# Attention block: probabilities scaled by the reciprocal of their sum, gate rows summed by four matmuls into one tile, last output tile in two column parts

## The chip, the cores and the metric

The kernel runs on one core of a Trainium2 chip. The metric is the device time of one execution in microseconds; the figure compared is the median over runs. A core has TensorE (PE, matmuls; PEld is its weight load), VectorE (DVE), ScalarE (ACT), GpSimd (POOL), and SyncE (SP), which issues the transfers here.

## The reference

One layer of a hybrid block with 2048 channels, 512 latent tokens and 256 context tokens. One input projection feeds eight heads of a gated delta rule (a scan) and eight heads of attention (two key/value heads, 768 keys). Both outputs are multiplied by a SiLU gate and pass through one output projection; its result, times a gate row, is added to x, and a final RMSNorm follows.

```python
def attend(q_blk, k_all, v_all):
    s = jnp.einsum('bqkgd,bskd->bkgqs', q_blk, k_all) * (HEAD_DIM ** -0.5)
    p = jax.nn.softmax(s, axis=-1)
    return jnp.einsum('bkgqs,bskd->bqkgd', p, v_all)

mod = jax.nn.silu(c) @ w_ada[l] + b_ada[l]
shift, scale, gate = jnp.split(mod, 3, axis=-1)          # 2048 channels each
...
attn_lat = block_attention(qa, k_all, v_all) * jax.nn.silu(z_a)
y = jnp.concatenate([gdn_lat, attn_lat], axis=-1) @ w_out
x = x + gate * y
return rms_norm(x, final_norm_w)
```

## The kernel before

Float32 products are built from two parts of each factor: hi is the value rounded to the matmul's format (a cast on ACT), lo the rest (a subtraction on DVE), and a product is three matmuls (hi hi, hi lo, lo hi), which is the helper mm3. Each weight piece of 256 KB is loaded by SP (wraw), cast on ACT (whi, L129), and its rest formed on DVE (wlo, L130). Names follow: whi_z and wlo_z belong to the gate projection z, whi_wo and wlo_wo to the output projection.

The program has a prologue (context and latent normalised, the modulation formed), the scan of the delta rule up to about 876 us, the attention stage from about 876 to 1114 us, then the output projection in four column blocks of 512, with four token tiles of 128 rows in each. The change lies in the attention stage and in the last column block.

The attention stage runs over units u = 0 to 16. Unit u = 2h + qp takes head h and the 256 queries qp; even units have qp = 0, odd ones qp = 1. Here "its unit" is the one whose scores are made, and "the unit before" is the one whose probabilities are used. In a unit stand, in the order of the code:

- attn_pt for the unit before: the probabilities pr (128 queries x 768 keys, two tiles) are transposed on PE, in three groups (pt), and each is split on ACT (pth) and DVE (ptl).
- attn_scores: the scores s in PSUM, and the row maximum on DVE (mx).
- attn_spread for the unit before: a matmul of ones with the diagonal tile dg puts 1/sum of each query on all partitions (ov), and ACT copies it to SBUF.
- attn_exp: two ACT operations make pr from s, with the sum of each row as their second output.
- fill(FS, 2): four steps of the generator of z matmuls (zl, 512 columns, three per step), and two steps of the gate row. A step of z matmuls at the start of a piece issues the casts and subtractions of a later weight piece. A step of the gate row (gate_rows) multiplies a 256 KB piece of w_ada by a scalar per partition and adds it to gacc on DVE (L1402).
- fill(FV, 2), then attn_values for the unit before: 18 matmuls of 256 columns (o), and on DVE the product of o, of ov and, where the gate of the head is known already ("early": M then holds it), of M.
- for the first five units the tanh and SiLU of a gate made earlier (zae, L1455).
- at an even unit attn_norm of the next head's queries (the copy qn, L1230); at an odd unit attn_qt: the next head's queries transposed (qtp) and split into qTh (ACT, L950) and qTl (DVE, L951), which the next unit's scores need.
- attn_over: the reciprocal of the row sums and dg, both on DVE.

PSUM tiles pt, ov, qtp share a ring of two places. The z matmuls and the sums of the gate row share another (pl).

The order of ACT, DVE and POOL in this stage is the order of the code (a manual schedule), and PE's has been written out too; SP issues its loads as their buffers come free. Every 512 columns of the gate row, gate_out sums gacc over the 128 partitions with a matmul of ones into 32 partitions (gater), adds the bias row on DVE and writes the 2 KB to memory (grd): three times inside the stage, from the z filler, once at its end. The epilogues read grd back as gbc.

In the last column block, for each token tile t, po3 is 48 matmuls of 512 columns; the epilogue multiplies by gbc (tt), adds x (yx), squares with a sum (fss) and multiplies by the final norm's weight fwb. Then DVE reduces the four sums, POOL takes the power -0.5 (fr), ACT and DVE scale one half of the row (1024 columns) each, and SP writes each half.

Of the kernel before, what the change touches and what calls it, by code (L numbers as in the profile page):

```python
# [68 lines left out]
def build(tc, a):  # L69
# [1202 lines left out]
            prs.append(pr)  # L1272
        return prs

    def attn_over(h, qp, mx):

        dg = ap_.tile([128, 2, 128], F32, tag="dg", bufs=2, name=f"dg{h}_{qp}")
        V.reciprocal(mx[:, 1], mx[:, 1])
        V.tensor_tensor(out=dg, in0=ident.unsqueeze(1).to_broadcast([128, 2, 128]),
                        in1=mx[:, 1].unsqueeze(2).to_broadcast([128, 2, 128]), op=ALU.mult)  # L1280
        return dg

    def attn_pt(h, qp, prs, j2):

# [8 lines left out]
        split_from(tp3, pth, ptl)  # L1293
        return pth, ptl

    def attn_spread(h, qp, dg):

        ov = ttile([128, 256], f"ov{h}_{qp}")
        T.matmul(ov, lhsT=ones, rhs=dg.rearrange("p a b -> p (a b)"), start=True, stop=True)
        over = ap_.tile([128, 256], F32, tag="ov", bufs=2, name=f"ov{h}_{qp}")  # L1300
        S.copy(over, ov)
        return over

    def attn_values(h, qp, pts, over):
        kv = h // 4
        op = PSt.tile([128, 256], F32, tag="o", name=f"o{h}_{qp}")
        for j in range(6):
            vsl = slice(kv * 128, kv * 128 + 128)
            mm3(op, vah[:, j, vsl], val[:, j, vsl], pts[j // 2][0][:, j % 2], pts[j // 2][1][:, j % 2], j == 0, j == 5)
        m = M[8 + h][:, qp * 256:qp * 256 + 256]  # L1310
        if (h, qp) in early:
            V.scalar_tensor_tensor(out=m, in0=m, scalar=0.5, in1=over, op0=ALU.mult, op1=ALU.mult)
# [31 lines left out]
    def fillers():  # L1344

        pieces = [z_piece(0), z_piece(1)]
        over = None
        yield
        for n in range(4 * len(zs)):
            i, kq = zs[n // 4], n % 4  # L1350
            if n + 2 < 4 * len(zs):
                pieces.append(z_piece(n + 2))
            if kq == 2 and outs:
                gate_out(*outs.pop(0))
            hi, lo = pieces.pop(0)
            if kq == 0:
                pl = PP.tile([128, SEQ], F32, tag="pl", name=f"zl{i}")
            for k4 in range(4):
                k = kq * 4 + k4
                for m, (lw, rt) in enumerate(((hi[:, k4], hhL[:, k]), (hi[:, k4], hl(0, k)), (lo[:, k4], hhL[:, k]))):  # L1360
                    T.matmul(pl, lhsT=lw, rhs=rt, start=k == 0 and m == 0, stop=k == KT - 1 and m == 2,  # L1361
                             skip_group_check=True)
# [6 lines left out]
    def gate_out(c, acc, row):

        pr = PP.tile([128, 512], F32, tag="pl", name=f"gater{c}")
        T.matmul(pr[0:32], lhsT=ones[:, 0:32], rhs=acc, start=True, stop=True)
        V.tensor_tensor(out=row, in0=row, in1=pr[0:1], op=ALU.add)
        SY.dma_start(grd[:, c * 512:c * 512 + 512], row)

    outs = []

    def gate_rows():

        def load(i):  # L1380
            c, k = divmod(i, KT)
            raw = ap_.tile([128, 512], F32, tag="graw", bufs=GB, name=f"graw{i}")
            SY.dma_start(raw, w_ada[k * 128:(k + 1) * 128, 2 * D + c * 512:2 * D + c * 512 + 512])
            return raw

        def bias(c):
            row = ap_.tile([128, 512], F32, tag="ze", bufs=2, name=f"grow{c}")[0:1]
            SY.dma_start(row, a["b_ada"][:, 2 * D + c * 512:2 * D + c * 512 + 512])
            return row

        raws = [load(i) for i in range(GB - 1)]
        acc = last = None
        yield
        for i in range(4 * KT):
            c, k = divmod(i, KT)
            raw = raws.pop(0)
            if k == 0:
                last, acc = acc, ap_.tile([128, 512], F32, tag="gacc", bufs=2, name=f"gacc{c}")
            if k == 0:
                V.tensor_scalar(out=acc, in0=raw, scalar1=scol[:, k:k + 1], scalar2=None, op0=ALU.mult)  # L1400
            else:
                V.scalar_tensor_tensor(out=acc, in0=raw, scalar=scol[:, k:k + 1], in1=acc, op0=ALU.mult, op1=ALU.add)  # L1402
            if i + GB - 1 < 4 * KT:
                raws.append(load(i + GB - 1))
            if k == 3 and c:
                outs.append((c - 1, last, bias(c - 1)))
            yield
        outs.append((3, acc, bias(3)))

    qcs = {i: attn_q(i) for i in (1, 2)}  # L1410
    for i in range(8):
# [21 lines left out]
    for u in range(2 * NH + 1):  # L1433
        h, qp = divmod(u, 2)
        more = h + 1 < NH
        prs, pts = None, []
        if before is not None:
            pts = [attn_pt(before[0], before[1], before[2], j2) for j2 in range(2)]
        if h < NH:
            sos, mx = attn_scores(h, qp, *qt, scs[h])  # L1440
        if before is not None:
            pts.append(attn_pt(before[0], before[1], before[2], 2))
            over = attn_spread(before[0], before[1], dg)
        if h < NH:
            prs = attn_exp(h, qp, sos, mx, scs[h])
            if qp == 1 and more:
                qn = next(qns)
            fill(FS + 5 * (before is None), 2)
        if before is not None:
            fill(FV, 2)  # L1450
            attn_values(before[0], before[1], pts, over)
        if u < NZA:

            e = ap_.tile([128, SEQ], F32, tag="ze", bufs=2, name=f"zae{u}")
            S.activation(e, M[8 + u], AF.Tanh, scale=0.5)  # L1455
            silu(V, M[8 + u], M[8 + u], e)
            early.update(((u, 0), (u, 1)))
        fill(FQ)
        if more:
            if qp == 0:  # L1460
                qns = attn_norm(h + 1, qcs.pop(h + 1))
                next(qns)
                if h + 3 < NH:
                    qcs[h + 3] = attn_q(h + 3)
            else:
                qt = attn_qt(h + 1, qn)
        if h < NH:
            dg = attn_over(h, qp, mx)
# [63 lines left out]
    for c in range(4):  # L1532
        cs_ = slice(c * 512, c * 512 + 512)
        for t in range(4):
            SY.dma_start(yx[:, t, cs_], a["x"][0, t * 128:t * 128 + 128, cs_])
        if c < 3:
            if c:
                ops = out_block(c)
            for t in range(4):
                epilogue(c, t, ops[t])  # L1540
            continue
        for k in range(KT):
            hi = op_.tile([128, 512], F32R, name=f"wlh{k}")
            lo = op_.tile([128, 512], F32R, name=f"wll{k}")
            raw = op_.tile([128, 512], F32, tag="rawl", bufs=2, name=f"rawl{k}")
            SY.dma_start(raw, w_out[k * 128:(k + 1) * 128, cs_])
            S.copy(hi, raw)
            V.tensor_tensor(out=lo, in0=raw, in1=hi, op=ALU.subtract)
            wlast.append((hi, lo))
        for t in range(4):  # L1550
            ts_ = slice(t * 128, t * 128 + 128)
            ps = PO.tile([128, 512], F32, tag="po", name=f"po3_{t}")
            for k in range(KT):
                mm3(ps, mh[k][:, ts_], ml[k][:, ts_], *wlast[k], k == 0, k == KT - 1)
            epilogue(c, t, ps)
            f = fr[:, t:t + 1]
            V.tensor_reduce(out=f, in_=fss[:, t], axis=AX.X, op=ALU.add)
            V.tensor_scalar(out=f, in0=f, scalar1=1.0 / D, scalar2=EPS, op0=ALU.mult, op1=ALU.add)
            power(f, -0.5)
            for q in range(2):  # L1560
                qs = slice(q * 1024, q * 1024 + 1024)
                if q == 0:
                    S.activation(yx[:, t, qs], yx[:, t, qs], AF.Copy, scale=f)
# [29 lines left out]
```

## Time and profile before

| what | value |
|---|---|
| runs | 1305.47, 1527.16 and 1306.19 us, median 1306.19 |
| profiled execution, own time | 1304.42 us |
| its span | 1302.6 us |
| mean granted TensorE clock | 0.993 |
| busy PE / PEld | 1250.4 us (96%) / 1018.4 us (78%) |
| busy DVE / ACT / POOL | 842.5 us (65%) / 583.4 us (45%) / 141.9 us (11%) |
| matmuls | 9226 |

The own time is that of the execution that was profiled; the span goes from its first to its last record. Rows of the order of time, below, read: start in us, duration in us, engine, source line, operation, output <- inputs, shapes, number of operations put together, and in brackets the idle time of the engine before it and what ended it. Grouped rows of waits read: engine and line that waited, for whom: us in total, times, longest. Rows of DMA issues read: count, KB each, us from issue to landing.

### The profile page before, as it was taken

How to read it: one execution, taken by the hardware profiler on the slowest of the kernel's cores; microseconds unless marked ns; L12 is line 12 of the kernel's file. 1: busy time of each engine (PE TensorE's matmuls, PEld its weight loads, DVE VectorE, ACT ScalarE, POOL GpSimd, SP SyncE). 2: the span in 40 equal slices, each digit the busy share in tenths (PEclk: the TensorE clock that was granted, in tenths of full speed). 3: DMA queues.
4: the chain of work that ended last, by engine and by line, in shares of the span. 5: the costliest groups of instructions: out<-in, count | busy, mean ns of one | idle time of the engine just before them, and what ended most of it. 6: DMA issues, size and time to landing. Idle time of an engine off the chain costs nothing. (4 is left out here: it accounts for less than half of the span.)

```text
span 1302.6 us, 24348 instructions
## 1 busy us (share of the span) xinstructions
PE 1250.4 (96%) x9226; PEld 1018.4 (78%) x9226; DVE 842.5 (65%) x1893; ACT 583.4 (45%) x1464; POOL 141.9 (11%) x206
## 2 busy tenths in 40 slices
PE   6799999999999999999999999999999999999997
PEld 4466688888888888888888877787888888788885
DVE  5444596686867678675776646537888887555432
ACT  4222363455545454544545444535555444434211
POOL 1323100111111111111111001100000000000000
PEclk9999999999999999999999999999999999999998
DMA  9999424231332313222132443356443443475302
GB/s 354 316 326 347 133 67 107 60 67 55 74 72 62 78 47 83 67 69 57 54 83 75 106 131 110 99 164 214 149 129 114 123 140 102 161 244 190 93 33 97
DMA packets 227000, 164.53 MB, mean 126 GB/s; under 512 B 62210, under 2 KB 198491, under 8 KB 225859
## 3 DMA queue, kind: packets, MB, share of 16 engines
q1 hardware_dynamic: 226586, 162.87, 42.9%
q8 instruction: 73, 1.20, 0.4%
q14 instruction: 44, 0.36, 0.1%
q10 hardware_dynamic: 297, 0.11, 0.0%
HBM read 148.85 MB, written 14.08 MB: 125 GB/s over the span
## 5 line engine op out<-in xcount | busy, mean ns | idle before, releaser
L240 POOL TENSOR_TENSOR sdh<-sth,egl 128x256 f32<-128x256 f32 x80 | 56.9, 711 | 446.6 <-DVE sth L892 344.8
L871 ACT ACTIVATE oqh<-ksh,egsw 64x128 f32<-64x128 f32 x128 | 46.3, 362 | 92.7 <-DVE rh L866 86.4
L866 DVE SCALAR_TENSOR_TENSOR rh<-ksh,negeg,vtokh 64x128 f32<-64x128 f32 x176 | 61.2, 348 | 31.1 <-PE ksh L854 24.5
L146 PE MATMUL po<-whi_wo,mh 128*128 128x512 f32 x192 | 76.2, 397 | 0.0
L148 PE MATMUL po<-whi_wo,ml 128*128 128x512 f32 x192 | 76.1, 396 | 0.0
L147 PE MATMUL po<-wlo_wo,mh 128*128 128x512 f32 x192 | 76.1, 396 | 0.0
L1361 PE MATMUL zl<-hhL,whi_z 128*128 128x512 f32 x176 | 74.0, 421 | 0.0
L1361 PE MATMUL zl<-hhL,wlo_z 128*128 128x512 f32 x176 | 69.8, 396 | 0.0
L1361 PE MATMUL zl<-hL,whi_z 128*128 128x512 f32 x176 | 69.6, 395 | 0.0
L130 DVE TENSOR_TENSOR wlo_wo<-wraw_wo,whi_wo 128x512 fp32r<-128x512 f32 x48 | 33.0, 690 | 55.5 <-ACT whi_wo L129 55.3
L886 PE MATMUL tsh<-vsh,ktok 128*128 128x128 f32 x352 | 56.6, 283 | 6.7 <-ACT vnh L882 3.5
L886 PEld LDWEIGHTS tsh<-vsh,ktok 128*128 128x128 f32 x352 | 47.4, 190 | 16.0 <-ACT vnh L882 7.9
L129 ACT CAST whi_wo<-wraw_wo 128x512 fp32r<-128x512 f32 x48 | 29.6, 620 | 67.3 <-PE po L148 56.8
L892 DVE TENSOR_TENSOR sth<-sdh,tsh 128x256 f32<-128x256 f32 x80 | 33.6, 420 | 27.4 <-PE tsh L886 19.2
L879 ACT ACTIVATE vsh<-tsh,cch 128x128 f32<-128x128 f32 x88 | 32.2, 366 | 38.4 <-PE tsh L875 37.1
L164 PE MATMUL vl<-hhL,wlo_v 128*128 128x512 f32 x112 | 46.3, 413 | 0.0
L164 PE MATMUL vl<-hhL,whi_v 128*128 128x512 f32 x112 | 46.2, 413 | 0.0
L164 PE MATMUL vl<-hL,whi_v 128*128 128x512 f32 x112 | 45.8, 409 | 0.0
L1402 DVE SCALAR_TENSOR_TENSOR gacc<-graw,scol,gacc 128x512 f32<-128x512 f32 x60 | 44.9, 748 | 1.0
L950 ACT CAST pth<-pt 128x512 fp32r<-128x512 f32 x48 | 26.8, 585 | 40.7 <-PE pt L1289 40.7
L146 PEld LDWEIGHTS po<-whi_wo,mh 128*128 128x128 f32 x192 | 36.2, 188 | 9.5 <-ACT whi_wo L129 0.8
L148 PEld LDWEIGHTS po<-whi_wo,ml 128*128 128x128 f32 x192 | 36.2, 189 | 8.7
(540 smaller groups left out, 3890.2 us busy)
## 6 DMA issues: line engine op xcount, KB each, us to landing
wada<-in_w_ada SPq DMA_DIRECT2D x64, 512.0 KB, 8.6
graw<-in_w_ada SPq DMA_DIRECT2D x64, 256.0 KB, 3.1
wraw_wo<-in_w_out SPq DMA_DIRECT2D x48, 256.0 KB, 3.3
wraw_z<-in_w_in SPq DMA_DIRECT2D x44, 256.0 KB, 3.1
wraw_v<-in_w_in SPq DMA_DIRECT2D x28, 256.0 KB, 2.9
wraw_k<-in_w_in SPq DMA_DIRECT2D x24, 256.0 KB, 2.9
wraw_q<-in_w_in SPq DMA_DIRECT2D x24, 256.0 KB, 2.8
xs<-in_x SPq DMA_DIRECT2D x4, 1024.0 KB, 5.4
```

What stands on the lines that cost most here:

```text
L130: (lo_eng or G).tensor_tensor(out=lo, in0=raw, in1=hi, op=ALU.subtract)
L146: T.matmul(out, lhsT=lh, rhs=rh, start=start, stop=False, skip_group_check=True)
L147: T.matmul(out, lhsT=lh, rhs=rl, start=False, stop=False, skip_group_check=True)
L148: T.matmul(out, lhsT=ll, rhs=rh, start=False, stop=stop, skip_group_check=True)
L164: T.matmul(out, lhsT=lw, rhs=rt[m], start=k == 0 and n == 0, stop=k == KT - 1 and n == 2, skip_group_check=True)
L240: eng.tensor_tensor(out=out, in0=x, in1=y, op=ALU.mult)
L866: V.scalar_tensor_tensor(out=r[rows], in0=ks[rows, d], scalar=gsc["negeg"][rows, gcol:gcol + 1], in1=vtok[rows, p], op0=ALU.mult, op1=ALU.add)
L871: S.activation(oq[rows, v, p - 2], ks[rows, d], AF.Copy, scale=gsc["egsw"][rows, gcol:gcol + 1])
L886: T.matmul(ts[:, d], lhsT=ktok[:, p, half], rhs=vs, start=True, stop=True, skip_group_check=True)
L892: V.tensor_tensor(out=sn, in0=sd, in1=ts[:, 0:2], op=ALU.add)
L1361: T.matmul(pl, lhsT=lw, rhs=rt, start=k == 0 and m == 0, stop=k == KT - 1 and m == 2, skip_group_check=True)
L1402: V.scalar_tensor_tensor(out=acc, in0=raw, scalar=scol[:, k:k + 1], in1=acc, op0=ALU.mult, op1=ALU.add)
```

## The change

Probabilities: attn_over and attn_spread become one function, attn_share, that takes the reciprocal and scales the two pr tiles in place on ACT. It stands behind fill(FS, 2), so in the unit that made the probabilities, and not behind attn_qt. The matmul ov, its copy, and dg are gone; attn_values uses o alone.

Gate rows: the four sums stay in four tiles gacc; the bias row is added on DVE to the first partition of gacc at the place where gate_out stood; one gate_out at the stage's end puts four matmuls into four bands of 32 partitions of one PSUM tile, which ACT copies whole and one transfer writes as 4 x 512.

Last token tile of the last block: two parts of 256 columns, each with 48 matmuls and its own epilogue; the square is taken of tt and not of yx; the sum of the row is finished by one operation behind the second part; its row is scaled and written in four pieces of 512 columns.

```diff
-    def attn_over(h, qp, mx):
-        dg = ap_.tile([128, 2, 128], F32, tag="dg", bufs=2, name=f"dg{h}_{qp}")
+    def attn_share(prs, mx):
         V.reciprocal(mx[:, 1], mx[:, 1])
-        V.tensor_tensor(out=dg, in0=ident.unsqueeze(1).to_broadcast([128, 2, 128]),
-                        in1=mx[:, 1].unsqueeze(2).to_broadcast([128, 2, 128]), op=ALU.mult)
-        return dg
+        for qi, pr in enumerate(prs):
+            S.activation(pr, pr, AF.Copy, scale=mx[:, 1, qi:qi + 1])
...
-    def attn_spread(h, qp, dg):
-        ov = ttile([128, 256], f"ov{h}_{qp}")
-        T.matmul(ov, lhsT=ones, rhs=dg.rearrange("p a b -> p (a b)"), start=True, stop=True)
-        over = ap_.tile([128, 256], F32, tag="ov", bufs=2, name=f"ov{h}_{qp}")
-        S.copy(over, ov)
-        return over
...
         if (h, qp) in early:
-            V.scalar_tensor_tensor(out=m, in0=m, scalar=0.5, in1=over, op0=ALU.mult, op1=ALU.mult)
-            mul(V, m, op, m)
+            V.scalar_tensor_tensor(out=m, in0=m, scalar=0.5, in1=op, op0=ALU.mult, op1=ALU.mult)
         else:
-            mul(V, m, op, over)
+            V.tensor_copy(m, op)
...
             if kq == 2 and outs:
-                gate_out(*outs.pop(0))
+                gate_bias(*outs.pop(0))
...
+    def gate_bias(acc, row):
+        V.tensor_tensor(out=acc[0:1], in0=acc[0:1], in1=row, op=ALU.add)
+
+    def gate_out(accs):
+        pr = PP.tile([128, 512], F32, tag="pl", name="gater")
+        for c, acc in enumerate(accs):
+            T.matmul(pr[32 * c:32 * c + 32], lhsT=ones[:, 0:32], rhs=acc, start=True, stop=True, skip_group_check=True)
+        row = ap_.tile([128, 512], F32, tag="ze", bufs=2, name="grow")
+        S.copy(row, pr)
+        SY.dma_start(grd.rearrange("o (c n) -> (o c) n", c=4), row[0:128:32])
...
             pts.append(attn_pt(before[0], before[1], before[2], 2))
-            over = attn_spread(before[0], before[1], dg)
         if h < NH:
             prs = attn_exp(h, qp, sos, mx, scs[h])
...
             fill(FS + 5 * (before is None), 2)
+            attn_share(prs, mx)
         if before is not None:
             fill(FV, 2)
-            attn_values(before[0], before[1], pts, over)
+            attn_values(before[0], before[1], pts)
...
-        if h < NH:
-            dg = attn_over(h, qp, mx)
         fill(FR)
...
     for o_ in outs:
-        gate_out(*o_)
+        gate_bias(*o_)
+    gate_out(accs)
...
+            else:
+                fl = op_.tile([128, 2], F32, name="fl")
+                for q in range(2):
+                    hs = slice(q * 256, q * 256 + 256)
+                    ws = slice(c * 512 + q * 256, c * 512 + q * 256 + 256)
+                    ps = PO.tile([128, 256], F32, tag="po", name=f"po3_{t}_{q}")
+                    for k in range(KT):
+                        hi, lo = [w[:, hs] for w in wlast[k]]
+                        mm3(ps, mh[k][:, ts_], ml[k][:, ts_], hi, lo, k == 0, k == KT - 1)
+                    tt = op_.tile([128, 512], F32, tag="tt", bufs=2, name=f"tt{c}_{t}_{q}")
+                    y = yx[:, t, ws]
+                    mul(V, tt[:, 0:256], ps, gbc[:, ws])
+                    V.tensor_tensor(out=tt[:, 0:256], in0=y, in1=tt[:, 0:256], op=ALU.add)
+                    S.activation(tt[:, 256:512], tt[:, 0:256], AF.Square, accum_out=fl[:, q:q + 1])
+                    mul(V, y, tt[:, 0:256], fwb[:, ws])
+                    if q == 0:
+                        ... (sum of the first parts, into f)
+                V.scalar_tensor_tensor(out=f, in0=fl[:, 1:2], scalar=1.0 / D, in1=f, op0=ALU.mult, op1=ALU.add)
             power(f, -0.5)
-            for q in range(2):
-                qs = slice(q * 1024, q * 1024 + 1024)
-                if q == 0:
+            n = 1024 if t < 3 else 512
+            for q in range(D // n):
+                qs = slice(q * n, q * n + n)
+                if q % 2 == 0:
                     S.activation(yx[:, t, qs], yx[:, t, qs], AF.Copy, scale=f)
```

The rows below are the instructions of an engine in the order of its queue: line, operation, output <- inputs (with buffer numbers), shape. On ACT, in unit 3 (head 1, second half of the queries), before the change, from the two exponentials to the cast that follows the queries' split:

```order
L1270 ACTIVATE pr_1_0_10552,mx_1_10536<-s_1_10523,mx_1_10536,hss_10180 128x768
L1270 ACTIVATE pr_1_1_10554,mx_1_10536<-s_1_10523,mx_1_10536,hss_10180 128x768
L129 CAST whi_z_2_10562<-wraw_z_2_10560 128x512
L1323 ACTIVATE ze_10576<-zl_10285 128x512
L129 CAST whi_z_3_10591<-wraw_z_3_10589 128x512
L1455 ACTIVATE zae_10631<-M_10042 128x512
L950 CAST qTh_10642<-qtp_10637 128x512
```

The same stretch of ACT after the change:

```order
L1270 ACTIVATE pr_1_0_10538,mx_1_10526<-s_1_10513,mx_1_10526,hss_10183 128x768
L1270 ACTIVATE pr_1_1_10540,mx_1_10526<-s_1_10513,mx_1_10526,hss_10183 128x768
L129 CAST whi_z_2_10548<-wraw_z_2_10546 128x512
L1312 ACTIVATE ze_10562<-zl_10284 128x512
L1279 ACTIVATE pr_1_0_10538<-pr_1_0_10538,mx_1_10526 128x768
L1279 ACTIVATE pr_1_1_10540<-pr_1_1_10540,mx_1_10526 128x768
L129 CAST whi_z_3_10580<-wraw_z_3_10578 128x512
L1449 ACTIVATE zae_10619<-M_10042 128x512
L950 CAST qTh_10630<-qtp_10625 128x512
```

The two scalings (L1279) came in ahead of the cast of weight piece 3; they read the reciprocal, which DVE writes into mx. On DVE in the same unit, before the change, from a step of the gate row to the diagonal:

```order
L1402 SCALAR_TENSOR_TENSOR gacc_10125<-graw_10435,scol,gacc_10125 128x512
L130 TENSOR_TENSOR wlo_z_3_10592<-wraw_z_3_10589,whi_z_3_10591 128x512
L1402 SCALAR_TENSOR_TENSOR gacc_10125<-graw_10441,scol,gacc_10125 128x512
L1402 SCALAR_TENSOR_TENSOR gacc_10125<-graw_10571,scol,gacc_10125 128x512
L1312 SCALAR_TENSOR_TENSOR M_10040<-M_10040,ov_0_10550 128x256
L240 TENSOR_TENSOR M_10040<-o_0_10610,M_10040 128x256
L237 SCALAR_TENSOR_TENSOR M_10042<-zae_10631,M_10042 128x512
L951 TENSOR_TENSOR qTl_10643<-qtp_10637,qTh_10642 128x512
L1278 RECIPROCAL mx_1_10536<-mx_1_10536 128x2
L1279 TENSOR_TENSOR dg_1_10646<-cmain,mx_1_10536 128x256
```

The same stretch of DVE after the change:

```order
L1396 SCALAR_TENSOR_TENSOR gacc_10125<-graw_10429,scol,gacc_10125 128x512
L1277 RECIPROCAL mx_1_10526<-mx_1_10526 128x2
L130 TENSOR_TENSOR wlo_z_3_10581<-wraw_z_3_10578,whi_z_3_10580 128x512
L1396 SCALAR_TENSOR_TENSOR gacc_10125<-graw_10435,scol,gacc_10125 128x512
L1396 SCALAR_TENSOR_TENSOR gacc_10125<-graw_10557,scol,gacc_10125 128x512
L1302 SCALAR_TENSOR_TENSOR M_10040<-M_10040,o_0_10599 128x256
L237 SCALAR_TENSOR_TENSOR M_10042<-zae_10619,M_10042 128x512
L951 TENSOR_TENSOR qTl_10631<-qtp_10625,qTh_10630 128x512
```

The reciprocal went from behind qTl to ahead of the weight piece's rest (wlo_z_3), the diagonal is gone, and one operation on M stands where two stood. On PE at the end of the stage, before the change, from the last z matmul to the first of the output projection:

```order
L1361 MATMUL zl_12437<-hhL,wlo_z_3_12490 128x512
L1372 MATMUL gater_12555<-gacc_11954,cmain 32x512
L146 MATMUL po_0_12572<-whi_wo_0_12580,mh_10026 128x512
L147 MATMUL po_0_12572<-wlo_wo_0_12581,mh_10026 128x512
L148 MATMUL po_0_12572<-whi_wo_0_12580,ml_10027 128x512
```

The same place of PE after the change:

```order
L1350 MATMUL zl_12358<-hhL,wlo_z_3_12407 128x512
L1365 MATMUL gater<-gacc_10125,cmain 32x512
L1365 MATMUL gater<-gacc_10723,cmain 32x512
L1365 MATMUL gater<-gacc_11313,cmain 32x512
L146 MATMUL po_0_12494<-whi_wo_0_12502,mh_10026 128x512
```

Three of the four sums stand together; the fourth stands 13 matmuls of the output projection later. The copy of the whole tile stands on ACT behind six casts of M (mh) and ahead of the cast of the fourth piece of w_out. On POOL the order is the same.

More of the change, by code (lines that the diff above doesn't have):

```diff
@@ L1294, in attn_pt, with attn_values @@
         return pth, ptl
-    def attn_spread(h, qp, dg):
-        ov = ttile([128, 256], f"ov{h}_{qp}")
-        T.matmul(ov, lhsT=ones, rhs=dg.rearrange("p a b -> p (a b)"), start=True, stop=True)
-        over = ap_.tile([128, 256], F32, tag="ov", bufs=2, name=f"ov{h}_{qp}")
-        S.copy(over, ov)
-        return over
-    def attn_values(h, qp, pts, over):
+    def attn_values(h, qp, pts):
         kv = h // 4
@@ L1367, in fillers @@
         z_over(*over)
[L1369 to L1376, printed above, removed]
+    def gate_bias(acc, row):
[7 more added lines that the diff above has]
+        SY.dma_start(grd.rearrange("o (c n) -> (o c) n", c=4), row[0:128:32])
+    outs, accs = [], []
     def gate_rows():
@@ L1391, in gate_rows @@
         raws = [load(i) for i in range(GB - 1)]
-        acc = last = None
         yield
@@ L1397, in gate_rows @@
             if k == 0:
-                last, acc = acc, ap_.tile([128, 512], F32, tag="gacc", bufs=2, name=f"gacc{c}")
+                acc = ap_.tile([128, 512], F32, name=f"gacc{c}")
+                accs.append(acc)
             if k == 0:
@@ L1405, in gate_rows @@
             if k == 3 and c:
-                outs.append((c - 1, last, bias(c - 1)))
+                outs.append((accs[c - 1], bias(c - 1)))
             yield
-        outs.append((3, acc, bias(3)))
+        outs.append((acc, bias(3)))
     qcs = {i: attn_q(i) for i in (1, 2)}
@@ L1551, in build @@
             ts_ = slice(t * 128, t * 128 + 128)
[L1552 to L1555, printed above, removed]
             f = fr[:, t:t + 1]
-            V.tensor_reduce(out=f, in_=fss[:, t], axis=AX.X, op=ALU.add)
-            V.tensor_scalar(out=f, in0=f, scalar1=1.0 / D, scalar2=EPS, op0=ALU.mult, op1=ALU.add)
+            if t < 3:
+                ps = PO.tile([128, 512], F32, tag="po", name=f"po3_{t}")
+                for k in range(KT):
+                    mm3(ps, mh[k][:, ts_], ml[k][:, ts_], *wlast[k], k == 0, k == KT - 1)
+                epilogue(c, t, ps)
+                V.tensor_reduce(out=f, in_=fss[:, t], axis=AX.X, op=ALU.add)
+                V.tensor_scalar(out=f, in0=f, scalar1=1.0 / D, scalar2=EPS, op0=ALU.mult, op1=ALU.add)
+            else:
[4 more added lines that the diff above has]
+                    ps = PO.tile([128, 256], F32, tag="po", name=f"po3_{t}_{q}")
+                    for k in range(KT):
+                        hi, lo = [w[:, hs] for w in wlast[k]]
[7 more added lines that the diff above has]
+                    if q == 0:
+                        V.tensor_reduce(out=f, in_=fss[:, t, 0:3], axis=AX.X, op=ALU.add)
+                        V.tensor_tensor(out=f, in0=f, in1=fl[:, 0:1], op=ALU.add)
+                        V.tensor_scalar(out=f, in0=f, scalar1=1.0 / D, scalar2=EPS, op0=ALU.mult, op1=ALU.add)
+                V.scalar_tensor_tensor(out=f, in0=fl[:, 1:2], scalar=1.0 / D, in1=f, op0=ALU.mult, op1=ALU.add)
```

## Prediction

> **What bounds the kernel now.** I read the page first, then the busy time of the stretch that the change touches, then the waits of PE in it, and last the order of time on DVE, ACT and PE around one of these waits. The profiled execution has a span of 1302.6 us:
>
> ```profile
> span 1302.6 us, 24348 instructions
> 876.00:1114.00 238.00, 232.84 (x1299) 194.57 (x1297) 187.25 (x311) 116.52 (x261) 8.49 (x7) 1.00 0.45 138
> PE pt L1289 <- DVE qTl L951: 3.0, 3, 1.2
> ```
>
> The second row is the attention stage (length; busy PE, PEld, DVE, ACT, POOL; granted clock 1.00). PE is busy in 232.84 of 238 us, DVE in 187.25, ACT in 116.52. Of its waits the largest group is for DVE's qTl: 3.0 us in 3 waits, the longest 1.2. So PE bounds the stage, and DVE is late in a few places. One is the end of unit 3 (the unit for head 1, queries 256 to 511):
>
> ```profile
> 927.30 0.74 DVE L1402 SCALAR_TENSOR_TENSOR gacc<-graw,scol,gacc 128x512 f32<-128x512 f32 x1
> 927.97 0.68 DVE L130 TENSOR_TENSOR wlo_z<-wraw_z,whi_z 128x512 fp32r<-128x512 f32 x1
> 928.57 1.53 DVE L1402 SCALAR_TENSOR_TENSOR gacc<-graw,scol,gacc 128x512 f32<-128x512 f32 x2
> 930.02 0.42 DVE L1312 SCALAR_TENSOR_TENSOR M<-M,ov 128x256 f32<-128x256 f32 x1
> 930.54 0.42 DVE L240 TENSOR_TENSOR M<-o,M 128x256 f32<-128x256 f32 x1
> 930.88 0.68 DVE L237 SCALAR_TENSOR_TENSOR M<-zae,M 128x512 f32<-128x512 f32 x1
> 931.48 0.69 DVE L951 TENSOR_TENSOR qTl<-qtp,qTh 128x512 fp32r<-128x512 f32 x1
> ...
> 923.97 0.19 ACT L1270 ACTIVATION_READ_ACCUMULATOR pr<-s,mx,hss 128x1 f32 x1
> 925.06 0.62 ACT L129 CAST whi_z<-wraw_z 128x512 fp32r<-128x512 f32 x1
> ...
> 932.22 0.66 PE L1289 MATMUL pt<-cmain,pr 128*128 128x128 f32 x4 [1.22 <-DVE qTl L951]
> ```
>
> DVE has no gap in these rows, and PE's second group of transposes waits 1.22 us until qTl, the last of them, has ended: the PSUM ring of pt, ov and qtp has two places, and qtp holds one until qTl is done. At such a place a microsecond more on DVE is a microsecond more on the kernel. ACT has time: its last cast of a weight piece begins at 925.06, 2.9 us before the DVE operation that reads it.
>
> **The change, term by term.** *The scaling of the probabilities.* The new order puts, on DVE, the reciprocal behind the gate-row step of 927.30 and ahead of wlo_z; on ACT, the two scalings of pr (128x768) ahead of the cast that this wlo_z reads. The exponentials have long ended (924.2), so the reciprocal starts when DVE reaches it, at 928.04, and ends at 928.2. A scaling of 768 columns from SBUF to SBUF does not stand in the trace. The nearest rows are the cast of 512 columns, 0.62, and a scaling of 1024 columns at the program's end, 1.15 (quoted with the tail). On the line between the two it is 0.89, and two of them, with the 0.1 by which neighbours on ACT overlap, take 1.7. They end at 929.9, the cast at 930.5, and wlo_z starts at 930.5 where it started at 927.97: **2.55 late**. Behind wlo_z stand two gate-row steps, the M operations and qTl, with no gap to absorb it; M<-M,ov goes (0.52, from 930.02 to 930.54). So qTl is 2.05 late, and so is PE.
>
> Where does the same hold? Unit 0 has no unit before it. In the other even units the next transposes read what ACT and DVE have long made (the three waits for qTl all stand at the end of odd units: 1, 3 and 9), so there I take the scaling as hidden. Of the odd units, 1, 3 and 9 pay 2.05. In 11 and 15 there is no M<-M,ov to remove (their heads are not yet gated): 2.55 each. The three others start from slack:
>
> ```profile
> 959.34 0.69 DVE L951 TENSOR_TENSOR qTl<-qtp,qTh 128x512 fp32r<-128x512 f32 x1 [0.64 <-ACT qTh L950]
> 959.93 1.03 PE L1289 MATMUL pt<-cmain,pr 128*128 128x128 f32 x8
> 986.25 0.69 DVE L951 TENSOR_TENSOR qTl<-qtp,qTh 128x512 fp32r<-128x512 f32 x1
> 986.83 1.04 PE L1289 MATMUL pt<-cmain,pr 128*128 128x128 f32 x8
> 1070.98 0.69 DVE L951 TENSOR_TENSOR qTl<-qtp,qTh 128x512 fp32r<-128x512 f32 x1 [1.17 <-ACT qTh L950]
> 887.63 0.56 ACT L1230 COPY qn<-qtp 128x512 f32<-128x512 f32 x1
> 885.23 1.29 DVE L130 TENSOR_TENSOR wlo_z<-wraw_z,whi_z 128x512 fp32r<-128x512 f32 x2
> ```
>
> In unit 5 DVE idles 0.64 ahead of qTl, which ends at 960.03; PE's eight transposes begin at 959.93, the second four some 0.4 later, 0.3 behind qTl: 2.05 - 0.64 - 0.3 = 1.1. Unit 13 idles 1.17; with 0.3 on PE as in unit 5 and no operation removed it pays 2.55 - 1.47 = 1.1. Unit 7 (986.94 against 986.83 + 0.4) has the 0.3 alone: 1.75. Sum 3 x 2.05 + 2 x 2.55 + 1.1 + 1.1 + 1.75 = **+15.2**. Unit 0: the reciprocal stands behind the pair of wlo_z that ends at 886.5, the scalings end near 888.4, a tanh of 0.6 follows, and the copy of qn, for which PE's transposes wait, comes at about 889.0 where it came at 887.63: **+1.4**.
>
> The bounds: a scaling takes 0.62 at least and 1.15 at most by the rows, so a unit's delay is 0.55 less or 0.5 more. Over eight units that is -4.5 to +4.
>
> *The spread matmuls that go.*
>
> ```profile
> 906.90 0.60 PE L1299 MATMUL ov<-dg,cmain 128*128 128x256 f32 x2
> 907.58 0.40 PE L1361 MATMUL zl<-hL,whi_z 128*128 128x512 f32 x1
> 907.81 0.40 PE L1361 MATMUL zl<-hhL,wlo_z 128*128 128x512 f32 x1
> ```
>
> Two passes (x2) for each of 16 blocks of queries. From the first pass to the second matmul behind it are 0.68 us, where one matmul at the usual step (907.58 to 907.81) would have taken 0.23: 0.45 each. Where an odd unit ends in a wait for qTl, PE only comes to it earlier; so just the eight even units earn it: **-3.6**. Their copies on ACT and dg on DVE go as well, off the path.
>
> *The gate rows.* Four sums go, of which three stood in the stage and one at its end:
>
> ```profile
> 1020.43 1.04 PE L1372 MATMUL gater<-gacc,cmain 128*32 128x512 f32 x2
> 1113.19 1.04 PE L1372 MATMUL gater<-gacc,cmain 128*32 128x512 f32 x2
> ...
> 44.90 1.92 PE L355 MATMUL ada<-wada,cs 128*32 128x512 f32 x16
> ```
>
> One takes about 1.0. Only that of 1020.43 lies in an even unit; those in units 5 and 13 come out of time that PE will wait through. At the end, three stand together and the fourth 13 matmuls later. What matmuls of 32 rows into four bands cost side by side is seen in the prologue: 16 passes in 1.92 us, 0.24 for a two-pass product, so three in a row cost what one alone costs (their passes run beside each other), about 1.0. I take -1.0 in the stage, -1.0 for the old one at the end, +1.0 for the three and +1.0 for the fourth: **0**. At worst the three run one after another, +2.0. The bias additions on DVE go on, into the sum and not behind it; the copy of 128x512 on ACT has six casts ahead and a cast of a weight behind it, and PE has 48 po matmuls of a piece to do meanwhile, 0.23 each or 11 us. If that cover is short, 0.6. The write to grd is read only by the epilogues, many microseconds on. SP issues three small writes less in the stage.
>
> Stage and its end: 15.2 + 1.4 - 3.6 = **+13.0**.
>
> *The tail.*
>
> ```profile
> 1292.51 0.39 PE L148 MATMUL po<-wlh,ml 128*128 128x512 f32 x1
> 1292.93 0.69 DVE L240 TENSOR_TENSOR tt<-po,gbc 128x512 f32<-128x512 f32 x1 [6.31 <-PE po L148]
> 1293.66 0.69 DVE L1528 TENSOR_TENSOR yx<-yx,tt 128x512 f32<-128x512 f32 x1
> 1294.45 0.63 ACT L1529 ACTIVATE tt<-yx 128x512 f32<-128x512 f32 x1 [7.42 <-DVE yx L1528]
> 1296.00 0.15 DVE L1558 TENSOR_SCALAR fr<-fr 128x1 f32<-128x1 f32 x1
> 1296.23 0.55 POOL L234 TENSOR_TENSOR fr<-fr,expo 128x1 f32<-128x1 f32 x1 [10.39 <-DVE fr L1558]
> 1296.81 1.15 ACT L1563 ACTIVATE yx<-yx,fr 128x1024 f32<-128x1024 f32 x1 [1.64 <-POOL fr L234]
> 897.36 0.28 PE L146 MATMUL o<-pth,vah 128*128 128x256 f32 x1
> 899.40 0.29 PE L148 MATMUL o<-pth,val 128*128 128x256 f32 x1
> out_y<-yx SPq DMA_DIRECT2D x8, 512.0 KB, 2.7
> o_d<-och SPq DMA_DIRECT2D x8, 256.0 KB, 2.0
> ```
>
> Two column parts make 96 matmuls of 256 columns of 48 of 512. The o matmuls, 18 from 897.36 to 899.40, step at 0.12; matmuls of 512 columns step at 0.23, as the zl above: 96 x 0.12 - 48 x 0.23 = +0.5, and the last one ends 0.1 earlier (0.28 for 0.39): +0.4. From the last matmul's end (1292.90) to the scaling (1296.81) are 3.91. With 256 columns the two DVE operations take 0.42 instead of 0.69 and the square about 0.38 instead of 0.63: -0.8. From the square's end (1295.08) to POOL's start (1296.23) are 1.15, in which DVE multiplies by fwb, sums and scales; the multiplication leaves the chain and the sum and the scaling become one operation, 0.15 and two hand-overs of 0.1: -0.8. So -1.6. Then come four scalings of 512, two on each of ACT and DVE (0.62 + 0.62 for 1.15 on ACT), and writes of 256 KB, which land in 2.0 where 512 KB land in 2.7, but four to issue: I take -0.2, of -0.7 to +0.3. The tail: 0.4 - 1.6 - 0.2 = **-1.4**, of -2.4 to 0.
>
> **Sum:** 13.0 - 1.4 = +11.6 on the execution's own 1304.42, which is 1316.0. The median of the runs shown lies 1.8 above that execution: 1306.19 + 11.6 = **1317.8**. The unknown sizes give its own range: 1312 to 1323.
>
> **Rivals.**
> 1. *The scalings hide everywhere*, because ACT reaches them earlier than I say. PE's work alone then counts: 16 x 0.45 of ov and two of the four gate sums go, 7.2 + 2.0, and the tail's 1.4: -10.6, 1295.6, not slower. For it: ACT's 49% in the stage, and the exponentials end 4 us earlier. Against it: the reciprocal stands behind DVE's queue, which had no gap in unit 3. It decides where the reciprocal runs before about 925.5. Chance 0.07.
> 2. *DVE runs ahead.* Without M<-M,ov (0.52) and dg (0.42) it reaches the reciprocal some 0.9 earlier, if nothing in between makes it wait, and each of the eight odd units pays 0.9 to 1.0 less: 15.2 becomes about 7.5, the time 1310 (1306 to 1312). Against it: DVE waits for PE's scores in each unit, which sets its start anew. Chance 0.14.
> 3. *Long waits halve PE's clock.* The waits of units 1, 3, 9, 11 and 15 become the old one plus the delay plus ov's 0.45: in unit 3 it is 1.22 + 2.05 + 0.45 = 3.7. The prologue has one of this size:
>
> ```profile
> 38.80 0.66 PE L422 MATMUL klat<-hhL,whi_w 128*128 128x512 f32 x1 [3.49 <-ACT hhL L399]
> 40.00:42.00 2.00, 1.84 (x5) 1.57 (x6) 2.00 (x4) 0.92 (x3) 1.21 (x1) 0.50 1.08 364
> ```
>
> Behind a wait of 3.49 us the granted clock (the 0.50) is half, for about 3.45 us, which loses 1.7. With three such units 1317.8 becomes 1322.9; if all eight odd units lose it, 1331.4, slower than before. Against it: my waits lie on both sides of 3.5. Chance 0.15, most of it below 1328. [...]
> 4. *The three gate sums don't run side by side*: +2.0, 1319.8, inside the forecast's range.
>
> **How the numbers follow.** The forecast's case, 1312 to 1323, has 0.60; rivals 0.07, 0.14 and 0.15; 0.04 is left for what I don't see. A range of 1306 to 1328 leaves out rival 1, a third of rival 3 and the rest. Two per cent (26 us, about what a measurement tells from no change) are passed below 1280 by next to nothing, 0.01, and above 1332 by the far end of rival 3 and the rest: 0.05.
>
> **What would show it.** Right: at the end of odd units PE's second pt waits 2 to 4 us for qTl; DVE's wlo_z waits some 2.4 us for whi_z; a scaling takes 0.89; the stage ends some 13 us later; three gate sums fill about 1 us; from the last po matmul to the span's end it is 1.8 shorter. Wrong: waits for qTl of 1 us as now, or scalings that start before the reciprocal's neighbours end, or a clock under 1.00 in the stage.

## The result, and the profile after

The changed kernel takes 1328.94 us (median of four runs, 1326.02 to 1330.1) beside 1306.65 before: a ratio of 1.017, 95% interval 1.0148 to 1.0192. One of the four runs before, 1527.16 us, stands far from the others and is not in the ratio. It is slower by 22 us, about twice what was forecast, and one microsecond above the range. The profiled execution has an own time of 1326.02 and a span of 1324.2.

The first view is the page's first line, then the attention stage (876 to 1135 now) in the columns of the row shown before, then PE's waits in it:

```profile
span 1324.2 us, 24356 instructions
876.00:1135.00 259.00, 233.11 (x1263) 197.31 (x1261) 177.99 (x285) 137.73 (x277) 7.04 (x7) 0.95 0.42 126
PE pt L1287 <- DVE qTl L951: 20.8, 7, 3.9
PE pt L1287 <- DVE ptl L951: 4.0, 2, 3.8
```

The stage is 21 us longer and its granted clock is 0.95 where it was 1.00. PE waits 24.8 us for DVE in it, where it waited 4.7. The place shown before, the end of unit 3, now reads:

```profile
932.05 0.74 DVE L1396 SCALAR_TENSOR_TENSOR gacc<-graw,scol,gacc 128x512 f32<-128x512 f32 x1
932.71 0.16 DVE L1277 RECIPROCAL mx<-mx 128x2 f32<-128x2 f32 x1
932.96 1.77 ACT L1279 ACTIVATE pr<-pr,mx 128x768 f32<-128x768 f32 x2 [3.04 <-DVE mx L1277]
934.63 0.60 ACT L129 CAST whi_z<-wraw_z 128x512 fp32r<-128x512 f32 x1
935.26 0.69 DVE L130 TENSOR_TENSOR wlo_z<-wraw_z,whi_z 128x512 fp32r<-128x512 f32 x1 [2.40 <-ACT whi_z L129]
937.32 0.41 DVE L1302 SCALAR_TENSOR_TENSOR M<-M,o 128x256 f32<-128x256 f32 x1
938.26 0.68 DVE L951 TENSOR_TENSOR qTl<-qtp,qTh 128x512 fp32r<-128x512 f32 x1
939.00 0.87 PE L1287 MATMUL pt<-cmain,pr 128*128 128x128 f32 x4 [3.68 <-DVE qTl L951]
```

The bracket of wlo_z names the cast, and the cast stands behind the two scalings: DVE is idle 2.40 us. PE then waits 3.68 us for qTl, where it waited 1.22. All of this is as the prediction has it. What follows on PE is the second loss. The next rows are the windows behind seven of the waits; the third number from the end is the granted clock:

```profile
905.20:912.00 6.80, 5.49 (x21) 4.80 (x21) 4.24 (x8) 0.58 (x1) 0.00 (x0) 0.50 0.31 83
939.20:942.60 3.40, 3.40 (x14) 3.07 (x13) 1.63 (x3) 0.58 (x1) 0.00 (x0) 0.52 0.43 129
970.00:973.40 3.40, 3.40 (x12) 2.80 (x11) 1.13 (x2) 0.57 (x1) 0.00 (x0) 0.50 0.47 136
1028.10:1031.40 3.30, 3.04 (x11) 2.75 (x12) 2.09 (x4) 0.58 (x1) 0.00 (x0) 0.50 0.57 164
1058.80:1062.20 3.40, 3.07 (x12) 2.78 (x13) 2.17 (x4) 0.58 (x1) 0.00 (x0) 0.50 0.83 242
1089.50:1092.90 3.40, 3.40 (x14) 3.07 (x13) 1.58 (x3) 0.58 (x1) 0.00 (x0) 0.50 0.61 185
1120.20:1123.60 3.40, 3.16 (x10) 2.68 (x11) 2.14 (x5) 0.58 (x1) 0.00 (x0) 0.50 0.09 31
```

PE ran at half clock for 27 us and was busy for 25 of them. Matmuls of 512 columns step at 0.43 us in the first of these windows (s, from 910.41 to 910.84) and at 0.23 behind it (zl, from 912.30 to 912.53). So at full clock that work takes about half the time, and up to 12.5 us are lost here.

The balance can be closed from the two profiles. The stage runs from the last zal4a matmul of the scan's end to the first po matmul. The rows of a tile give count, duration (min, median, max in ns), first and last start; first of before, then of after:

```profile
L164 PE MATMUL zal4a<-hhL,wlo_z4a x16: 393/399/400, 865.7 to 876.2; 128*128 128x512 f32 x16
L146 PE MATMUL po<-whi_wo,mh x192: 389/397/499, 1114.2 to 1248.3; 128*128 128x512 f32 x192
...
L164 PE MATMUL zal4a<-hhL,wlo_z4a x16: 393/399/399, 865.2 to 875.7; 128*128 128x512 f32 x16
L146 PE MATMUL po<-whi_wo,mh x192: 389/397/497, 1135.4 to 1270.7; 128*128 128x512 f32 x192
```

Before, the stage is 1114.2 - 876.2 = 238.0 us; after, 1135.4 - 875.7 = 259.7: +21.7. From the first po matmul to the end of the span it is 188.4 before and 188.8 after, and the part ahead of the stage is 0.5 shorter. Together 21.6, the difference of the two own times. Within the stage, the waits for DVE bring +20.1 and unit 0 some 0.7; the spread matmuls take away 16 x 0.45 = 7.2 and three gate sums of 1.07 another 3.2. What is left, 21.7 - 20.8 + 10.4 = 11.3, fits the half clock. The 0.45 of a spread matmul is the prediction's figure; no run has these matmuls gone and nothing else changed.

### The profile page after: what moved, and what is told of

It reads as the page before. It is cut to its first block, busy times and chain, and to the rows that moved or that the text cites. A ratio compares the mean times of both kernels' runs of the same rounds, so it can differ in the third digit from the quotient of the medians.

```text
span 1324.2 us, 24356 instructions
## 1 busy us (share of the span) xinstructions
PE 1254.2 (95%) x9242; PEld 1025.5 (77%) x9242; DVE 834.3 (63%) x1873; ACT 605.9 (46%) x1484; POOL 140.4 (11%) x206
## 5 line engine op out<-in xcount | busy, mean ns | idle before, releaser
L1287 PE MATMUL pt<-cmain,pr 128*128 128x128 f32 x192 | 31.0, 294 | 25.9 <-DVE qTl L951 20.8
L130 DVE TENSOR_TENSOR wlo_z<-wraw_z,whi_z 128x512 fp32r<-128x512 f32 x44 | 30.3, 690 | 39.8 <-ACT whi_z L129 39.8
L1287 PEld LDWEIGHTS pt<-cmain,pr 128*128 128x128 f32 x192 | 24.3, 150 | 33.4 <-DVE qTl L951 22.4
```

Source lines behind the costliest of these rows:

```text
L130: (lo_eng or G).tensor_tensor(out=lo, in0=raw, in1=hi, op=ALU.subtract)
L1287: T.transpose(out=tp3[:, jj, qi * 128:qi * 128 + 128], in_=prs[qi][:, j * 128:j * 128 + 128], identity=ident)
```

## The experiments

Theory A: the scalings delay a cast, the cast delays qTl, and the idle time on PE also halves its clock. Rival B: the gate rows or the tail are to blame. Rival C: the clock's fall costs nothing of its own. Rival D: the scalings are too much for ACT wherever they stand.

**The scaled probabilities alone** (gate rows and tail as before):

```diff
+            attn_share(prs, mx)          # on the kernel before; attn_over, attn_spread, dg, ov gone
```

> The kernel before with the scaled probabilities alone; gate rows and last token tile as before. Theory A (the scalings stand on ACT ahead of the cast of a weight piece, so qTl comes 2 to 2.5 us late at the end of odd units, PE waits 2 to 4 us there, and these waits halve its clock): all the loss is here, some 1330 us, seven or so waits of 2 to 4 us for qTl and a mean clock near 0.98. Rival B (the loss comes from the gate rows or the tail, and the waits for qTl are paid back): under 1318.

It took 1327.75 us beside 1307.19 before (1.0157, 1.014 to 1.0174). This part alone is 20.6 us slower; rival B falls. Its stage, between the same two marks, is 256.8 us long, and the waits are those of the changed kernel, with two exceptions: the gate sums that still stand in units 5 and 13 fill 1.2 us of theirs. Only four units are followed by half clock. The wait of unit 15 is not, though it is longer than most of those that are:

```profile
1122.20 0.66 PE L1287 MATMUL pt<-cmain,pr 128*128 128x128 f32 x4 [3.82 <-DVE ptl L951]
1120.00:1122.00 2.00, 0.00 (x0) 0.00 (x0) 1.97 (x4) 0.00 (x0) 0.00 (x0) 1.00 0.34 81
1122.00:1124.00 2.00, 1.79 (x10) 1.57 (x11) 1.23 (x3) 0.59 (x1) 0.00 (x0) 1.00 0.15 58
```

So the length of a wait alone does not decide. The section on the hardware comes back to this.

**PE kept busy in the waits.** The same delay, but PE has something to do in it:

```diff
+                if j2 == 1 and qp == 0:          # ahead of the transposes that wait for qTl
+                    sp = PSs.tile([128, 2 * NTOK], F32, tag="s", name=f"s{h}_{qp}")
+                    for _ in range(17):
+                        T.matmul(sp[:, 0:256], lhsT=kTh[:, 0, 0:128], rhs=kTh[:, 0, 0:256], start=True, stop=True, ...)
```

> The changed kernel with 17 matmuls of 256 columns (17 x 0.12 = 2.0 us) ahead of each group of transposes that waits for qTl; they write into the scores' tile, which the scores then overwrite, and nothing reads them. They fill time in which PE waits anyway. Theory A: the idle rests are 1.9 us at most, the clock stays at 1.00 in the stage, and the kernel gains what the half clock cost, some 12 us: about 1316. Rival C (the clock's fall is a by-product and the time lies in the delay alone): no gain, 1328 or a little more.

It took 1318.5 us (1.0088, 1.0071 to 1.0104), 2.5 over what theory A gave, and 10 us less than the changed kernel, with 136 matmuls more. The first rows are its waits, the third is its stage, with a clock of 1.00:

```profile
PE pt L1288 <- DVE qTl L951: 6.7, 6, 1.9
PE pt L1288 <- DVE ptl L951: 1.9, 2, 1.8
876.00:1127.50 251.50, 241.79 (x1414) 206.93 (x1412) 178.95 (x286) 138.90 (x279) 7.05 (x7) 1.00 0.44 132
```

The waits are 16.2 us shorter (8.6 for 24.8), which is the time of the fillers, eight times 2.0: DVE is as late as it was, and the delay is still paid. What the fillers gave back is the half clock. Rival C falls. The figure lies beside the forecast's: 1317.8 was the sum for a kernel that pays the delay and keeps its clock.

**Fewer fillers, so that waits of 1 to 3 us remain** (8 in place of 17):

> The changed kernel with 8 instead of 17 idle-filling matmuls (0.96 us) at each place that waits for qTl. The delay on DVE is the same, so the waits left are about 2.9, 2.7, 1.5, 1.0, 2.1, 2.1, 1.5 and 2.9 us. Theory A1 (a free-running window of 3.41 us with some 2.05 us of idle time or more halves the clock, one with 1.9 or less does not, so the phase decides for waits between 2 and 4 us): one to four of the waits over 2 us are followed by half clock, each costing some 1.7 us: 1320 to 1325, between the 1318.5 of 17 matmuls and the 1328.9 of none. Rival A2 (only waits of at least 3.4 us halve the clock): no half clock, 1318 to 1319.

It took 1323.62 us (1.0124, 1.0107 to 1.0142), inside theory A1's range. The profiled execution is the shortest of the four, 1319.82 us at a mean clock of 0.989; the others took 1323.56 to 1324.66 at 0.987 to 0.984, so the same kernel meets half clock more or less often. In the profiled one, three of the five waits over 2 us are followed by it. Two of these are the shortest, 2.17 and 2.16 us; the longest, 2.94, is not one of them:

```profile
907.23 0.66 PE L1288 MATMUL pt<-cmain,pr 128*128 128x128 f32 x4 [2.94 <-DVE qTl L951]
937.16 1.12 PE L1288 MATMUL pt<-cmain,pr 128*128 128x128 f32 x4 [2.77 <-DVE qTl L951]
1024.86 0.66 PE L1288 MATMUL pt<-cmain,pr 128*128 128x128 f32 x4 [2.17 <-DVE qTl L951]
1055.75 0.66 PE L1288 MATMUL pt<-cmain,pr 128*128 128x128 f32 x4 [2.16 <-DVE qTl L951]
1115.66 0.66 PE L1288 MATMUL pt<-cmain,pr 128*128 128x128 f32 x4 [2.86 <-DVE ptl L951]
```

A rule by which a wait has to last 3.4 us (rival A2, 1318 to 1319) falls.

**The delay alone, on the kernel before**, with ACT and the probabilities as they were:

```diff
+        dl = ap_.tile([128, 4, 128], F32, tag="dl", bufs=1, name=f"dl{h}")
+        for _ in range(4):
+            V.tensor_tensor(out=dl, in0=qn, in1=qn, op=ALU.add)
         split_from(tp.rearrange("p t c -> p (t c)"), *qt)
```

> The kernel before, with four additions of 128x512 (0.65 us each by the steps of such rows, 2.6 us) ahead of qTl on DVE at the end of seven odd units; their output is used by nothing. ACT and the probabilities are as before. By the waits of before, the delay alone is 2.6 us in units 1, 3 and 9 and less where there was slack, some 15 us: waits of 3.8, 3.8, 1.7, 2.3, 3.2, 2.5 and 1.1 us. Theory A (the delay and the idle time that it makes are the whole cause, whatever ACT does): half clock behind two to five of these waits, 1325 to 1330. Rival C: the delay alone, 1321 to 1322, and no half clock.

It took 1333.16 us (1.02, 1.0184 to 1.0216), 3 us over what theory A gave. The waits came a little longer than I had summed (4.48 and 4.36 in units 1 and 3), and five units are followed by half clock, one of them for two windows. One of the shorter waits shows the turn, with the windows ahead of and behind it:

```profile
1006.27 0.66 PE L1292 MATMUL pt<-cmain,pr 128*128 128x128 f32 x4 [2.20 <-DVE qTl L951]
1004.00:1007.50 3.50, 1.30 (x9) 1.09 (x9) 3.40 (x8) 1.06 (x2) 0.00 (x0) 1.00 0.26 100
1007.50:1010.90 3.40, 3.40 (x15) 3.00 (x14) 3.00 (x5) 0.12 (x1) 0.00 (x0) 0.50 0.29 80
```

So half clock follows PE's idle time here too, where additions on DVE make it and no scaling of probabilities is in the program.

**The scalings behind the cast.** If the place in ACT's queue is the cause, the same work in another place must cost far less:

```diff
             fill(FS + 5 * (before is None), 2)
-            attn_share(prs, mx)
+            V.reciprocal(mx[:, 1], mx[:, 1])
         if before is not None:
             fill(FV, 2)
+        if h < NH:
+            attn_share(prs, mx)          # now the two scalings alone
+        if before is not None:
             attn_values(before[0], before[1], pts)
```

> The changed kernel with the two scalings moved behind the cast of the second weight piece of the unit (behind the second filler on ACT); the reciprocal stays. Theory A: wlo_z no longer waits for the scalings, the waits for qTl go back to some 1.5 us, the clock stays at 1.00, and the work taken off PE (ov, three gate sums, the tail) shows: 1295 to 1300. Rival D (two scalings in each unit are too much for ACT wherever they stand, and the casts behind them come late): over 1312.

It took 1300.27 us (0.9947, 0.993 to 0.9964), just above the range that theory A gave and far from rival D's 1312. The same end of unit 3:

```profile
928.42 0.62 ACT L129 CAST whi_z<-wraw_z 128x512 fp32r<-128x512 f32 x1
931.32 0.16 DVE L1441 RECIPROCAL mx<-mx 128x2 f32<-128x2 f32 x1
931.39 0.67 DVE L130 TENSOR_TENSOR wlo_z<-wraw_z,whi_z 128x512 fp32r<-128x512 f32 x1
931.57 1.76 ACT L1278 ACTIVATE pr<-pr,mx 128x768 f32<-128x768 f32 x2 [2.54 <-DVE mx L1441]
934.50 0.68 DVE L951 TENSOR_TENSOR qTl<-qtp,qTh 128x512 fp32r<-128x512 f32 x1
935.24 0.66 PE L1286 MATMUL pt<-cmain,pr 128*128 128x128 f32 x4 [1.35 <-DVE qTl L951]
```

The cast now runs 3 us ahead of its reader, wlo_z follows the reciprocal at once, and the two scalings stand behind it. The stage is 1108.2 - 879.4 = 228.8 us long, 9.2 less than before.

**The other two parts.** The gate rows alone and the tail alone, on the kernel before:

> The kernel before with the gate rows summed by four matmuls at the end alone. Three sums of 1.07 us leave the stage and the fourth stands 13 matmuls into the output projection: -3.2 + 1.1 = -2.1, about 1305. Rival (my prediction's view that the sums in odd units are hidden in waits): 0, 1307.

1304.37 us beside 1306.56 (0.9981, 0.9972 to 0.9989): a gain of 2.2. The stage is 234.3 long, 3.7 less; behind it stands 1.2 more, the fourth sum. What three sums cost together is seen in the changed kernel's rows, six passes in the time that two take:

```profile
1134.44 1.06 PE L1365 MATMUL gater<-gacc,cmain 128*32 128x512 f32 x6
1138.62 1.05 PE L1365 MATMUL gater<-gacc,cmain 128*32 128x512 f32 x2
```

> The kernel before with the last token tile in two column parts alone. By my sum -1.4 us; by the profile of the changed kernel -0.7 (the end is 1.6 shorter, the matmuls some 0.9 longer, of which the fourth gate sum is not part here): 1305.5 to 1306.5 beside 1307.2. Rival: the two parts cost PE as much as the end saves, no difference.

1306.6 us beside 1306.56 (1.0, 0.999 to 1.001): no difference that can be measured. By its profile, about 1 us less from the first po matmul to the end (187.5 for 188.4), within the interval.

Gate rows and tail together, with the reciprocal, the diagonal and the spread matmul put back:

> The changed kernel with the reciprocal, the diagonal and the spread matmul put back; gate rows and last token tile as changed. Theory A: no long wait, the clock at 1.00, and a gain from the tail (1.4 us) and from gate sums that no longer stand in the stage (1 to 2 us): 1303 to 1305. Rival B: 1310 or more.

1304.26 us beside 1307.19 (0.9976, 0.9964 to 0.9988), as expected.

The parts do not add up: the probabilities alone bring +20.6 us, the other two together -2.9, and the changed kernel +22.3. The profiles show a reason. Without the gate sums the waits of units 5 and 13 are 2.51 us each where they are 1.31 with them, and both are then followed by half clock, which they are not when the probabilities are changed alone. A saving inside a stretch where PE waits was no saving, and made the wait long enough to cost more. Unit 15 is followed by half clock in the changed kernel alone, though its wait is the same in both (3.85 and 3.82 us); the section on the hardware takes that up.

**A further step.** In the kernel with the scalings behind the cast, one gate-row step of the second filler is moved from each odd unit to an even one, and then both:

```diff
-            fill(FV, 2)
+            fill(FV, 1 if qp else 3)     # and 0 if qp else 4
```

> The kernel with the scalings behind the cast (1300.3), and one step of the gate row moved from the second filler of each odd unit to that of an even unit (one and three steps instead of two and two). A gate-row step takes DVE 0.77 us ahead of qTl in odd units, where PE waits 0.6 to 1.4 us. If DVE's queue ahead of qTl is what PE waits for, the four waits for qTl shrink by 0.7 each or to nothing: about 1297.5. Rival: the even units have no room on DVE, waits for wlo_z or ptl appear there, and the time stays at 1300 or rises.

> As the kernel with one and three gate-row steps (1295.4), with none in the second filler of the odd units and four in that of the even ones. If DVE's queue is what the waits of 0.7 and 1.3 us for qTl come from, they vanish: 1293 to 1294.5. Rival: four gate-row loads follow each other too closely, or even units get too long on DVE, and the time is 1295 or more.

They took 1295.37 (0.992, 0.9903 to 0.9937) and 1296.2 (0.9911, 0.9895 to 0.9928, against the runs of before beside them). The first is below what was expected, 1297.5; the second misses its 1293 to 1294.5, and its rival holds. Between the marks of the stage the three kernels differ by less than the times say: 228.8 us with two steps each, 1104.2 - 877.1 = 227.1 and 1106.3 - 879.8 = 226.5 with the steps moved. So some 2 us lie where the edit acts; in the profile of the first another 2.3 lie ahead of the stage, where the two programs are the same. The waits for qTl fell from 4.1 to 2.8 and 2.4 us, not to nothing: in unit 3 the wait is 1.34 or 1.35 us in all three, so there qTl does not come late by the gate row. With no step of the second filler ahead of it (the second kernel), the trace names what is left in unit 3:

```profile
930.95 1.76 ACT L1278 ACTIVATE pr<-pr,mx 128x768 f32<-128x768 f32 x2 [2.54 <-DVE mx L1441]
932.62 0.62 ACT L1451 ACTIVATE zae<-M 128x512 f32<-128x512 f32 x1
933.26 0.69 DVE L237 SCALAR_TENSOR_TENSOR M<-zae,M 128x512 f32<-128x512 f32 x1 [1.49 <-ACT zae L1451]
933.87 0.69 DVE L951 TENSOR_TENSOR qTl<-qtp,qTh 128x512 fp32r<-128x512 f32 x1
```

The scalings now hold up the next operation on ACT, zae; DVE idles 1.49 us for it, and qTl stands behind. No run moves them behind zae as well.

## Why the prediction was wrong

**The step that failed is the half clock, a term that the sum put at nothing.** The prediction named it as rival 3, "Long waits halve PE's clock", with a price of 1.7 us a unit and waits of 3.7, and gave it a chance of 0.15, "most of it below 1328". The waits came as said. The term measured 11.3 us by the balance and 10.4 by the fillers, half of the whole loss; without it 1328.94 would be 1317.6. Seven of the eight odd units paid in the profiled execution, one of them twice: eight windows at some 1.4 us each, as PE waits in part of them.

The ground for setting it aside was wrong. I took one row of the trace, the wait of 3.49 us in the prologue, for a threshold near 3.5, and wrote that my waits lie on both sides of it. They need not reach it: waits of 2.16 us were followed by half clock, and one of 3.82 was not. The trace of before could have shown this, for the wait of 3.49 us was not the only one that half clock followed. These two rows of before are a wait of 2.06 us that ends at 160.59, and the window at half clock that begins 1.3 us later:

```profile
160.59 0.47 PE L164 MATMUL kvl<-hhL,whi_kv 128*128 128x512 f32 x1 [2.06 <-DVE craw L201]
161.86:165.27 3.41, 3.41 (x11) 2.73 (x10) 3.41 (x11) 3.41 (x4) 0.00 (x0) 0.50 0.04 13
```

**The delay** was right in place and size. The prediction had wlo_z 2.55 late (DVE idle 2.40 in unit 3), a scaling at 0.89 us (0.93), and waits that grow by the delay, by ov's 0.45, and in units 5 and 13 by the gate sum that goes: 15.2 + 8 x 0.45 + 2 x 1.0 = 20.8 us, where 20.1 came. Unit 0 was set at 1.4 and cost 0.7. Rivals 1 and 2 (hidden scalings; DVE running ahead) fell with that.

**The spread matmuls** fit the balance at the 0.45 that the prediction gave them. With the scalings behind the cast the stage is 5.7 us shorter than with gate rows and tail alone (228.8 beside 1115.0 - 880.5 = 234.5), where 7.2 would go if the waits stayed the same; those for DVE are 1 us longer.

**The gate rows** were summed to 0. In the changed kernel that was about right, as the two sums in odd units came out of waits. On the kernel before, where PE does not wait in units 5 and 13, they are worth -2.2. That three sums cost what one does was right (1.06). Rival 4 fell.

**The tail** was set at -1.4 and gives between -1.3 and +1.3, by the profiles about -1. The chain behind the last matmul:

```profile
1315.65 0.28 PE L148 MATMUL po<-wlh,ml 128*128 128x256 f32 x1
1317.49 0.16 DVE L1572 SCALAR_TENSOR_TENSOR fr<-fl,fr 128x1 f32<-128x1 f32 x1 [0.18 <-ACT tt L1566]
1318.32 1.33 ACT L1578 ACTIVATE yx<-yx,fr 128x512 f32<-128x512 f32 x2 [0.86 <-POOL fr L234]
1318.83 1.80 SPq L1581 DMA_DIRECT2D out_y<-yx  x4
```

From the last matmul's end (1315.93) to the scaling (1318.32) are 2.39, where I had 2.3. But from there to the span's end (1324.2) are 5.88, where before 1296.81 to 1302.6 were 5.79: the two scalings on ACT take 1.33 for 1.15, and SP needs 1.80 to issue its four transfers. My -0.2 for this was +0.1. With some 0.5 for the matmuls of the two parts (0.4 by my sum) that is -1.5 + 0.1 + 0.5 = -0.9.

## What to carry to other kernels

An operation on an engine with time to spare was not free here: ACT was busy in 116.52 of the stage's 238 us, and the same scalings gave 1328.94 us ahead of the cast and 1300.27 behind it, as the cast fed a chain that PE waited for. Put such an operation behind what others wait for, and check what it delays, not how busy its engine is. Here waits of PE that were 1.4 us at most grew to 1.9 to 3.9, and they counted twice: 20.1 us as idle time, and by the balance 11.3 as work at half clock behind them. When a change lengthens waits of PE, look in the trace for both. And before a single row of a trace is taken for a threshold, look through the same trace for a smaller one that already crosses it.

## What the runs showed of the hardware

In these runs the length of a wait of PE did not tell whether half clock followed: behind one of 2.16 us it did (8 fillers, unit 11), behind one of 3.82 it did not (scaled probabilities alone, unit 15). Cut into windows of 3.41 us, the idle time of PE tells the waits below apart. In the changed kernel half clock began at 905.2, 939.3, 970.0, 1028.1, 1058.8, 1089.5 and 1120.2; the steps are 10, 9, 17, 9, 9 and 9 times 3.41 us. Each stretch lasts 3.41 us, the first 6.83. Laid on a grid of this step, each wait can be cut into what falls in each window (the start of the half clock being the end of the window that set it):

| kernel and unit | wait, us | idle in one window of 3.41 us | half clock |
|---|---|---|---|
| scaled probabilities alone, unit 15 | 3.82 | 1.92, then 1.90 | no |
| 8 fillers, unit 1 | 2.94 | 1.88, then 1.06 | no |
| 8 fillers, unit 15 | 2.86 | 1.57, then 1.29 | no |
| delay alone, unit 3 | 4.36 | 1.95, then 2.40 | yes, two windows |
| scaled probabilities alone, unit 9 | 3.12 | 2.05 | yes |
| before, at 160.6 us | 2.06 | 2.06 | yes |
| 8 fillers, units 9 and 11 | 2.17, 2.16 | 2.17, 2.16 | yes, both |
| delay alone, unit 7 | 2.20 | 2.19 | yes |
| changed kernel, unit 5 | 2.51 | 2.51 | yes |
| changed kernel, unit 15 | 3.85 | 3.41 | yes |

In the attention stage of these runs the most idle time in a window of this table that half clock did not follow is 1.92 us, and the least that it did follow is 1.95. A wait of 2.16 us that fell into one window was followed by it; one of 3.82 that was split into 1.92 and 1.90 was not. Two windows that ran at half clock themselves were followed by another with less idle time: 1.34 us (changed kernel, unit 1) and 1.09 us (scaled probabilities alone, unit 1).

Two windows at the start of the changed kernel do not fit. The first and the third row are these windows, with 2.55 and 1.72 us of idle time; the second and the fourth are the windows behind them, and only the fourth is at half clock:

```profile
4.05:7.46 3.41, 0.86 (x4) 0.90 (x5) 0.00 (x0) 0.98 (x1) 0.00 (x0) 1.00 1.01 395
7.46:10.87 3.41, 3.41 (x18) 3.21 (x17) 2.78 (x9) 1.88 (x3) 0.55 (x1) 1.00 1.02 416
21.12:24.53 3.41, 1.69 (x12) 0.48 (x10) 2.69 (x10) 1.63 (x4) 0.55 (x1) 1.00 1.10 348
24.53:27.95 3.42, 1.97 (x9) 0.31 (x10) 0.29 (x1) 0.00 (x0) 0.55 (x1) 0.50 1.10 348
```

So the idle time that the profile shows does not tell all windows apart; what else does stays open.
